# In a split-precision encoder block, operand groups are loaded behind the next weight pieces, and the work after each item gets a deadline

## The chip, the cores and the metric

The kernel runs on one core of one Trainium2 chip. The metric is device time in microseconds (us). The engines are named as in the profile: PE does matrix products (PEld is its weight load), DVE and ACT work on tiles, POOL and SP here issue transfers; L235 is line 235 of the kernel. "SPq", "POOLq" and "ACTq" stand for a transfer being issued by that engine's sequencer.

## The reference

One block of a streaming encoder over 512 tokens with 2048 channels, all in float32. An input projection feeds two mixers (a gated linear recurrence, mLSTM, and a short gated convolution), whose results go through two branch products, are merged by gates, and go through an output product; then a gated MLP of width 5504, with a short convolution between its products:

```python
hn = rmsnorm(h, norm_mix_g)
proj = hn @ w_in + b_in                                  # 2048 -> 11272
y_m = gate(mlstm(q, k, v, i, f)) @ w_branch_m            # 1024 -> 2048
y_c = (cb * causal_dwconv(cc * ch, conv_w)) @ w_branch_c # 1024 -> 2048
h = h + (sigmoid(gm) * y_m + sigmoid(gc) * y_c) @ w_out  # 2048 -> 2048
u = causal_dwconv(rmsnorm(h, norm_ffn_g) @ w_up, ffn_conv_w, ffn_conv_b)  # 2048 -> 2 * 5504
h = h + (silu(gate) * val) @ w_down                      # 5504 -> 2048
return rmsnorm(h, norm_out_g)
```

## The kernel before

Every large product is done in blocks by a seven-product (Strassen) scheme, and each float32 operand is split in two parts that PE can multiply: a high part (`hi`, an ACT copy) and the remainder (`lo`, a DVE subtraction). One product is then three matmuls, high by high (L279), high by low (L280) and low by high (L281), each 128x128 by 128x256.

The program is a list of **steps**. A step uses one **weight piece** (1 MB of combined weights in a slot of the ring `raw`): two halves, seven products each, 42 matmuls. An **item** is a run of steps (`q` = 0 to `nq` - 1) whose results collect in one set of PSUM banks; two items are interleaved at the start and at the end of each phase. The phases follow the reference: the input projection, `w_bc`, `w_bm`, `w_out`, `w_up`, `w_down` in three chunks of the inner width, and a short rest. I count pieces from 0 in a phase: `w_down.0` is the first of `w_down`. The phases meet at about 905 (into `w_bc`), 1060 (into `w_out`), 1245 (into `w_up`), 2140 (into `w_down`, first chunk), 2330 and 2455 us (second and third chunk).

**A weight piece** needs: two 128 KB loads on SP (L250, L251), two 128 KB loads on POOL that are added onto the first two once these have landed (L253), a 512 KB load on SP (L260); two sums on DVE (L216, L221); two high parts on ACT (L231); two low parts on DVE (L235), the second of which is the last use of the slot. In the last piece of some items ("eight") only the 512 KB load is there, the high parts are L184 and L185, the low parts L189 and L190.

**An operand group** (`cell_task`, `direct_cell`) is the activation side of a phase: two 256 KB loads of intermediate results from DRAM (L326), sums on DVE (L342 to L352; in `direct_cell` with L386 and L387 ahead), the high part on ACT (L356) and the low part on DVE (L359), which frees the slot. There are eight buffers (`ACTS`) for the finished groups, so the groups of a new phase are made while PE works at the seam of two phases, one every step or two.

Weight pieces and operand groups share the six slots of `raw` (`RAW`). `order` is the list of all of them in load order. SP works through it in that order: the n-th load is issued when the (n - 6)-th in the list has been used up. The list is made of `tasks[k]`, one list per step; an operand group whose work is to be done around step `k` is put ahead of weight piece `k`.

When an item ends, ACT copies the shared bank out (`evac_first`, L303) and DVE adds the other banks into a tile `z` (L309 to L312, `evac_ops`). Then come its **posts** (normalise, convolve, gate, store), put into the queue `posts` and worked off a few at a time when a running `credit` of DVE time allows. `flush` runs what is left of an older item's posts in one go when a later item ends, ahead of its L303: they read the tile `z` that L303 writes next. In the `up` phase the posts are L686 and L838 to L853 and the store into `a_d` (L148, issued by ACT); in the `down` phase L864 on ACT and an adding store into `h_d` (L155, issued by POOL).

Of the kernel before, what the change touches and what calls it, by code (L numbers as in the profile page):

```python
# [44 lines left out]
def kpair(c):  # L45

    q, r = divmod(c, 2)
    return 4 * q + r, 4 * q + 2 + r
# [12 lines left out]
class Task:  # L61


    def __init__(self, load, sums, hi, lo, ready=None):
        self.load, self.sums, self.hi, self.lo, self.ready = load, sums, hi, lo, ready
        self.wh = self.wl = None
        self.raw, self.cost, self.plain, self.after_end, self.pre = None, (0.8, 2.05), False, None, None


@with_exitstack  # L70
def tile_block(ctx: ExitStack, tc: tile.TileContext, xT, w1, w_v0, w_v1, w_v2, w_bm, w_bc, w_out, w_up, w_down,
# [13 lines left out]
    def nm(s):  # L85
        uid[0] += 1
        return f"{s}_{uid[0]}"
# [227 lines left out]
    def cell_task(xs, c, d, scale=None, key=None, eight=False):  # L315

        k1, k2 = kpair(c) if isinstance(c, int) else c
        t = Task(None, None, None, None)

        def new_raw():  # L320
            t.raw = wp.tile([P, NW], F32, tag="raw", name=nm("xraw"), bufs=RAW)

        def load():
            new_raw()
            for dst, k in zip(t.two(), (k1, k2)):
                SP.dma_start(dst, d[k])  # L326

        def two_k():
            return (t.raw[:, :T], t.raw[:, T:2 * T]) if eight else (t.raw[:, 5 * SW:], t.raw[:, :2 * SW])

        def scaled():
            for ap, k in zip(two_k(), (k1, k2)):
                A.activation(ap, ap, AF.Copy, scale=scale(k))

        def diff():
            x = slots(t.raw)
            V.tensor_sub(x[:, 4:6], x[:, 0:4:2], x[:, 1:4:2])

        def t3():
            x = slots(t.raw)  # L340

            V.tensor_sub(x[:, 2:4], x[:, 1:6:4], two(x[:, 6]))  # L342

        def e():

            x = slots(t.raw)
            V.scalar_tensor_tensor(x[:, 4], x[:, 3], -1.0, x[:, 1], op0=ALU.mult, op1=ALU.subtract)

        def t4():

            x = slots(t.raw)
            V.scalar_tensor_tensor(x[:, 6], x[:, 4], -1.0, x[:, 0], op0=ALU.mult, op1=ALU.subtract)  # L352

        def hi():
            t.act = actp.tile([P, 2 * NW], F32R, tag="act", name=nm("act"))
            A.activation(t.act[:, :m], t.raw[:, :m], AF.Copy)  # L356

        def lo():
            V.tensor_sub(t.act[:, NW:NW + m], t.raw[:, :m], f(t.act[:, :m]))  # L359
            t.raw = None  # L360
            xs[t.cell] = t.act
            t.act = None

        t.load, t.sums, t.hi, t.lo, t.new_raw = load, [diff] if eight else [t3, e, t4], hi, lo, new_raw
        t.two, m = two_k, 6 * SW if eight else NW
        t.pre = scaled if scale else None
        t.cost = (0.65, 1.7) if eight else (1.35, 1.95)
        t.ready = (lambda: all(k in stored for k in key)) if key else None
        return t

    def direct_cell(xs, c, it, d=None, scale=None, key=None, eight=False):

        t = cell_task(xs, c, d, None, key, eight)
        cell_t3, cell_load = t.sums[0], t.load
        k1, k2 = kpair(c)

        def load():
            if d is not None:
                cell_load()
            else:  # L380
                t.new_raw()

        def t3():
            assert it.done
            a, b = t.two()
            V.tensor_add(a, a, it.z[:, :T])  # L386
            V.scalar_tensor_tensor(b, it.z[:, T:], -1.0, b, op0=ALU.mult, op1=ALU.subtract)  # L387
            it.z_read = True
            cell_t3()

        def scaled():
            assert it.done
            for ap, z, k in zip(t.two(), (it.z[:, :T], it.z[:, T:]), (k1, k2)):
                A.activation(ap, z, AF.Copy, scale=scale(k))
            it.z_read = True

        it.z_read = False
        t.load = load
        if d is not None:
            t.sums = [t3] + t.sums[1:]  # L400
        else:
            t.pre = scaled
        t.cost = (t.cost[0] + (1.35 if d is not None else 0), t.cost[1])
        t.after_end = it
        return t
# [464 lines left out]
    steps, items_all, all_cells = [], [], []  # L870
# [190 lines left out]
    t = last_act()  # L1061
    t.cell, t.first, t.last, t.after, t.spread, t.xs = "x", e_last, e_last + 15, 0, e_last - 4, plain
    all_cells.append(t)
    n_main = len(steps)
    steps.extend((l, 0) for l in lasts)


    tasks = [[] for _ in range(len(steps) + 1)]
    wt = [weight_task(it, q) if isinstance(it, Item) else last_weight(it.n) for it, q in steps]
    k, cells_at = 0, {}  # L1070
    for n, t in enumerate(all_cells):
        if n < 8:
            k = t.cell
        else:
            k = max(k, all_cells[n - 8].last + 3, t.after, t.spread)
            if tasks[k]:
                k += 1
            t.k = k
            cells_at.setdefault(k, []).append(t)
            assert k <= t.first, (n, k, t.first)  # L1080
        tasks[k].append(t)
    for s, t in enumerate(wt):
        tasks[s].append(t)
    order = [t for ts in tasks for t in ts]
    place = {id(t): i for i, t in enumerate(order)}
    at = [place[id(t)] for t in wt] + [len(order) - 1] * 8
    n_load, n_lo, held = [0], [0], [0]

    def load_next():
        i = n_load[0]  # L1090
        if i == len(order) or i - n_lo[0] + held[0] == RAW or (order[i].ready and not order[i].ready()):
            return False
        order[i].load()
        n_load[0] += 1
        return True

    def loads():
        while load_next():
            pass
# [5 lines left out]
    def lo_ops(t):  # L1105

        def done():
            n_lo[0] += 1

        if isinstance(t.wh, list):  # L1110
            return [lambda: t.lo(0), lambda: (t.lo(1), done())]
        return [lambda: (t.lo(), done())]
# [123 lines left out]
    for i in range(at[START]):  # L1236
# [4 lines left out]
        while todo_mm:  # L1241
            s, r = todo_mm[0]
            it, q = steps[s]
# [41 lines left out]
    credit = 0.0  # L1285
    urgent = {it.num for it in items_all if it.urgent}


    finals, lq, lsum = deque(), [], []

    for s in range(START, len(steps)):
        it, q = steps[s]
# [89 lines left out]
        if s >= START + hold:  # L1382
            credit = min(credit, 2.5)
            rush = not main or any(x[0] in urgent for x in posts)
            for x in list(posts)[:2]:
                cost, fn = x[1][0]
                if not rush and cost and credit <= cost / 2:
                    break
                x[1].popleft()
                credit -= cost  # L1390
                fn()
                if not x[1]:
                    posts.remove(x)
        for t in cells_at.get(s + 3, []):
            if t.pre and t.raw is not None and (not t.after_end or t.after_end.done):
                t.pre()
                t.pre = None
# [10 lines left out]
        if not main and it.n > 11 and finals:  # L1408
            for _ in range(2):
                if finals:  # L1410
                    last_scale(0, finals.popleft(), row0)
        loads()
    for l in lq:
        last_post(l)
    for l in lsum + lq:
# [68 lines left out]
```

## Time and profile before

| | |
|---|---|
| time, median of 3 runs (lowest to highest) | 2645.81 us (2645.74 to 2651.76) |
| the profiled execution: its own time, its span | 2654.39 us, 2652.7 us |
| mean granted PE clock (1.00 is 2.4 GHz) | 0.99 |
| PE busy, share of the span, matmuls | 2584.3 us, 97%, 21146 |
| DVE, ACT, POOL busy | 2112.7, 1291.1, 796.4 us (80%, 49%, 30%) |
| DMA, mean over the span | 223 GB/s |

A matmul's duration in the trace is longer than its distance to the next one (they are pipelined): in undisturbed stretches one starts every 0.12 us. A stretch with n matmuls therefore has n x 0.12 us of work, and the rest of the stretch is lost, by waits or by a lower clock. Times in the views are counted from the start of the span.

### The profile page before, as it was taken

To read this page: it belongs to the slowest core of one execution; us is meant where nothing else is said; L and a number is where in the kernel's file an instruction comes from. 1 tells how busy PE (TensorE), PEld (TensorE's weight loads), DVE (VectorE), ACT (ScalarE), POOL (GpSimd) and SP (SyncE) were. 2 spreads that over 40 slices of the span, in tenths; PEclk is the share of its full clock that TensorE was granted. 3 is DMA by queue.
4 is the path that set the end of the run, shared out by engine and by line. 5 is a ranking of instruction groups with operands and counts; after the bars stand their busy time and mean duration, and the time that the engine had idled before them with its cause. 6 is when DMAs were issued, how large, how long until landed. Compare 5 with 4: busy or idle time off the path is not lost.

```text
span 2652.7 us, 55503 instructions
## 1 busy us (share of the span) xinstructions
PE 2584.3 (97%) x21146; PEld 2564.9 (97%) x21146; DVE 2112.7 (80%) x3308; ACT 1291.1 (49%) x1748; POOL 796.4 (30%) x922
## 2 busy tenths in 40 slices
PE   8999999999999999899999999999999989999998
PEld 8999999999999999899899999999999989999997
DVE  8577778886777888877989888888888887676756
ACT  6444554546556543345555445444444544444433
POOL 2443333333333111221333333333333223232320
PEclk8999999999999999999999999999999999999999
DMA  7798989998898797887998889989888888898976
GB/s 216 181 228 229 240 223 253 221 252 225 231 248 219 227 298 208 218 244 209 236 224 227 221 221 227 225 219 225 222 222 220 209 219 210 200 239 195 233 173 203
DMA packets 462557, 592.55 MB, mean 223 GB/s; under 512 B 42784, under 2 KB 296736, under 8 KB 462288
## 3 DMA queue, kind: packets, MB, share of 16 engines
q1 hardware_dynamic: 301968, 419.79, 50.4%
q0 software_dynamic: 133088, 124.04, 31.4%
q10 hardware_dynamic: 27232, 45.17, 4.7%
q8 instruction: 165, 2.70, 0.4%
q14 instruction: 104, 0.85, 0.1%
HBM read 531.17 MB, written 57.67 MB: 222 GB/s over the span
## 4 chain that ended last, share of the span: by engine, by line
PE 54%; DVE 6%; DMA 3%; issue 2%; ACT 0%; POOL 0%; DVEq 0%; SPq 0%; POOLq 0%; ACTq 0%
PE bank L281 18%; PE bank L279 18%; PE bank L280 17%; DMA raw<-in_w_down_dram 2%; DVE wl L235 1%; DVE act L359 1%; DMA raw<-in_w_out_dram 1%; DVE z L310 0%; PE bank L440 0%; PE bank L1164 0%; PE bank L1165 0%; PE bank L1166 0%; DMA raw<-in_w_up_dram 0%; DVE z L309 0%; DMA h_d<-z 0%
## 5 line engine op out<-in xcount | busy, mean ns | idle before, releaser
L281 PE MATMUL bank<-act,wl 128*128 128x256 f32 x6760 | 1922.7, 284 | 33.5 <-DVE wl L235 28.5
L279 PE MATMUL bank<-act,wh 128*128 128x256 f32 x6760 | 1931.1, 286 | 14.3 <-ACT z L303 5.8
L280 PE MATMUL bank<-act,wh 128*128 128x256 f32 x6760 | 1919.3, 284 | 0.0
L281 PEld LDWEIGHTS bank<-act,wl 128*128 128x128 f32 x6760 | 1303.9, 193 | 39.4 <-DVE wl L235 33.4
L279 PEld LDWEIGHTS bank<-act,wh 128*128 128x128 f32 x6760 | 1304.2, 193 | 18.8 <-ACT z L303 6.5
L231 ACT ACTIVATE wh<-raw 128x896 fp32r<-128x896 f32 x856 | 812.1, 952 | 1036.9 <-PE bank L280 679.5
L280 PEld LDWEIGHTS bank<-act,wh 128*128 128x128 f32 x6760 | 1304.3, 193 | 2.8 <-issue 1.7
L235 DVE TENSOR_TENSOR wl<-raw,wh 128x896 fp32r<-128x896 f32 x856 | 929.1, 1087 | 343.1 <-PE bank L281 231.7
L253 POOL DMA_DIRECT2D raw<-in_w_up_dram x344 | 298.5, 941 | 603.4 <-DMA raw<-in_w_up_dram 371.9
L253 POOL DMA_DIRECT2D raw<-in_w_dram x280 | 244.1, 961 | 527.1 <-DMA raw<-in_w_dram 344.9
L216 DVE TENSOR_TENSOR raw<-raw 128x256 f32<-128x256 f32 x428 | 179.6, 420 | 37.3 <-DMA raw<-in_w_down_dram 23.1
L253 POOL DMA_DIRECT2D raw<-in_w_down_dram x112 | 100.9, 1032 | 282.2 <-DMA raw<-in_w_down_dram 107.4
L221 DVE TENSOR_TENSOR raw<-raw 128x256 f32<-128x256 f32 x428 | 179.0, 418 | 0.3
L309 DVE TENSOR_TENSOR z<-bank,z 128x512 f32<-128x512 f32 x131 | 89.8, 686 | 38.4 <-ACT z L303 28.3
L356 ACT ACTIVATE act<-xraw 128x1792 fp32r<-128x1792 f32 (+1 forms) x52 | 85.6, 1646 | 60.2 <-DVE xraw L352 49.5
L184 ACT ACTIVATE wh<-raw 128x256 fp32r<-128x256 f32 x96 | 40.0, 416 | 131.0 <-PE bank L280 118.6
L359 DVE TENSOR_TENSOR act<-xraw,act 128x1792 fp32r<-128x1792 f32 (+1 forms) x52 | 101.7, 1955 | 0.0
L686 DVE TENSOR_TENSOR z<-z,rstd 128x1024 f32<-128x1024 f32 x83 | 100.8, 1217 | 0.2 <-ACT rstd L457 0.2
L189 DVE TENSOR_TENSOR wl<-raw,wh 128x256 fp32r<-128x256 f32 x96 | 40.5, 421 | 64.3 <-PE bank L281 37.3
L310 DVE TENSOR_TENSOR z<-bank,z 128x512 f32<-128x512 f32 x131 | 89.6, 684 | 1.7
L312 DVE TENSOR_TENSOR z<-bank,z 128x512 f32<-128x512 f32 x131 | 89.5, 683 | 0.0
L253 POOL DMA_DIRECT2D raw<-in_w_out_dram x48 | 41.8, 983 | 131.5 <-DMA raw<-in_w_out_dram 91.0
(214 smaller groups left out, 1380.3 us busy)
## 6 DMA issues: line engine op xcount, KB each, us to landing
raw<-in_w_up_dram SPq DMA_DIRECT2D x172, 512.0 KB, 5.7
raw<-in_w_dram SPq DMA_DIRECT2D x144, 512.0 KB, 5.9
raw<-in_w_up_dram SPq DMA_DIRECT2D x344, 128.0 KB, 3.9
raw<-in_w_up_dram POOLq DMA_DIRECT2D x344, 128.0 KB, 5.4
raw<-in_w_down_dram SPq DMA_DIRECT2D x80, 512.0 KB, 5.1
raw<-in_w_dram SPq DMA_DIRECT2D x280, 128.0 KB, 4.3
raw<-in_w_dram POOLq DMA_DIRECT2D x280, 128.0 KB, 5.4
raw<-in_w_out_dram SPq DMA_DIRECT2D x32, 512.0 KB, 5.2
```

The lines of the kernel that those rows point to most:

```text
L216: V.tensor_add(x[:, 6], x[:, 5], x[:, 0])
L221: V.tensor_add(x[:, 2], x[:, 6], x[:, 1])
L231: A.activation(seven(t.wh[r]), half(r), AF.Copy)
L235: V.tensor_sub(seven(t.wl[r]), half(r), seven(f(t.wh[r])))
L253: G.dma_start(at(i), a21, accum_op=ALU.add)
L279: PE.matmul(ps, h, xh, start=start, stop=False, skip_group_check=True)
L280: PE.matmul(ps, h, xl, start=False, stop=False, skip_group_check=True)
L281: PE.matmul(ps, l, xh, start=False, stop=stop, skip_group_check=True)
L309: return [lambda: V.tensor_add(z[:, 0:4:3], b0, two(z[:, 1])), lambda: V.tensor_add(z[:, 1:3], b1, two(z[:, 3])), lambda: V.tensor_add(z[: ...
L310: lambda: V.tensor_add(z[:, 1:3], b1, two(z[:, 3])),
L359: V.tensor_sub(t.act[:, NW:NW + m], t.raw[:, :m], f(t.act[:, :m]))
L686: V.tensor_mul(sb_pair(it.z), sb_pair(it.z), two(rstd))
```

## The change

Three edits. (1) In `order`, an operand group no longer stands ahead of the weight piece of its step `k` but `behind` steps later: 2 in general, 1 for groups from a load that are scaled first, 3 for groups that are made from `z` without a load. The step at which its work on DVE and ACT is done stays. Which loads may be issued is now counted along the list with a flag `done`, since groups and pieces may be used up out of the list's order. (2) A post is also run when its item's remaining posts are as many as the steps left until `due`, the end of the item whose evacuation needs the tile. (3) `loads()` stands ahead of two later parts of the loop's body. (`for t in cells_at.get(s + 3, [])` scales groups early on ACT.)

```diff
 class Task:
+        self.done, self.behind = False, 2
 def cell_task(...):
-        t.pre = scaled if scale else None
+        if scale:
+            t.pre, t.behind = scaled, 1
 def direct_cell(...):
         else:
-            t.pre = scaled
+            t.pre, t.behind = scaled, 3
...
-    k, cells_at = 0, {}
+    low, cells_at = 0, {}
     for n, t in enumerate(all_cells):
         if n < 8:
             k = t.cell
         else:
-            k = max(k, all_cells[n - 8].last + 3, t.after, t.spread)
-            if tasks[k]:
+            k = max(low, all_cells[n - 8].last + 3, t.after, t.spread)
+            if k in cells_at:
                 k += 1
-            t.k = k
+            t.k = low = k
             cells_at.setdefault(k, []).append(t)
             assert k <= t.first, (n, k, t.first)
+            k = min(k + t.behind, len(steps))
         tasks[k].append(t)
...
     def load_next():
         i = n_load[0]
+        while n_lo[0] < i and order[n_lo[0]].done:
+            n_lo[0] += 1
...
         def done():
-            n_lo[0] += 1
+            t.done = True
...
+    ends = {it.num: s for s, (it, q) in enumerate(steps[:n_main]) if q == it.nq - 1}
+
+    def due(num):
+
+        n = num + 2
+        return ends.get(n if n < len(items_all) and (n < 42 or items_all[n].pre) else n + 1, len(steps))
...
-                if not rush and cost and credit <= cost / 2:
+                if not rush and cost and credit <= cost / 2 and len(x[1]) < due(x[0]) - s:
                     break
...
+        loads()
         for t in cells_at.get(s + 3, []):
...
-        loads()
```

PE's rows stand in the same order before and after. Three places where others move are shown; lines of the kernel after are one or two higher.

**SP at the seam into `w_down`**, before: an operand group (from `a_d`), the last piece of `w_up`, a group, `w_down.0`, and the first two rows of `w_down.1`.

```order
L326 DMA xraw_25251<-a_d 128x512 x2
L250 DMA raw_25309<-in_w_up_dram 128x256
L251 DMA raw_25309<-in_w_up_dram 128x256
L260 DMA raw_25309<-in_w_up_dram 128x2x512
L326 DMA xraw_25315<-a_d 128x512 x2
L250 DMA raw_25375<-in_w_down_dram 128x256
L251 DMA raw_25375<-in_w_down_dram 128x256
L260 DMA raw_25375<-in_w_down_dram 128x2x512
L250 DMA raw_25439<-in_w_down_dram 128x256
L251 DMA raw_25439<-in_w_down_dram 128x256
L260 DMA raw_25439<-in_w_down_dram 128x2x512
```

The same place after:

```order
L251 DMA raw_25188<-in_w_up_dram 128x256
L252 DMA raw_25188<-in_w_up_dram 128x256
L261 DMA raw_25188<-in_w_up_dram 128x2x512
L327 DMA xraw_25254<-a_d 128x512 x2
L251 DMA raw_25312<-in_w_down_dram 128x256
L252 DMA raw_25312<-in_w_down_dram 128x256
L261 DMA raw_25312<-in_w_down_dram 128x2x512
L327 DMA xraw_25375<-a_d 128x512 x2
L251 DMA raw_25378<-in_w_down_dram 128x256
L252 DMA raw_25378<-in_w_down_dram 128x256
L261 DMA raw_25378<-in_w_down_dram 128x2x512
```

The groups shown before are the third and the fourth of this phase, and after the second and the third: the last piece of `w_up` and `w_down.0` each have two groups fewer ahead of them, and so come two places earlier in the ring. The same happens at the other seams; 74 rows of SP's list differ in all.

**DVE near 2195 us**, at the end of an item of `w_down`, before: low parts of a weight piece, then six posts of one item of `up` (L686 to L853 on `z_92`), and the evacuation of the next item, which writes `z_92` (L309).

```order
L235 TENSOR_TENSOR wl_26045<-raw_25829,wh_25971 128x896
L312 TENSOR_TENSOR z_93<-bank_86,z_93 128x512
L235 TENSOR_TENSOR wl_26048<-raw_25829,wh_26030 128x896
L686 TENSOR_TENSOR z_92<-z_92,rstd 128x1024
L842 SCALAR_TENSOR_TENSOR mB<-z_92,pcol,mB 128x511
L843 SCALAR_TENSOR_TENSOR mB<-z_92,pcol,mB 128x510
L846 SCALAR_TENSOR_TENSOR mB<-z_92,pneg,mB 128x511
L847 SCALAR_TENSOR_TENSOR mB<-z_92,pneg,mB 128x510
L853 TENSOR_TENSOR mB<-mB 128x512
L216 TENSOR_TENSOR raw_25897<-raw_25897 128x256
L309 TENSOR_TENSOR z_92<-bank_80,z_92 128x2x256
```

After, from the fourth row of the evacuation before it on:

```order
L236 TENSOR_TENSOR wl_26051<-raw_25829,wh_25972 128x896
L313 TENSOR_TENSOR z_93<-bank_86,z_93 128x512
L236 TENSOR_TENSOR wl_26054<-raw_25829,wh_26027 128x896
L848 SCALAR_TENSOR_TENSOR mB<-z_92,pneg,mB 128x511
L849 SCALAR_TENSOR_TENSOR mB<-z_92,pneg,mB 128x510
L855 TENSOR_TENSOR mB<-mB 128x512
L217 TENSOR_TENSOR raw_25959<-raw_25959 128x256
L310 TENSOR_TENSOR z_92<-bank_80,z_92 128x2x256
```

Between the last low part and the evacuation three posts are left; the other three (L686, L842 and L843 of before) stand earlier, ahead of the evacuation of `z_93`.

**ACT near 2212 to 2235 us**, in the same chunk, before: L864 (the `down` post) of `z_93`, then high parts, and L864 of `z_92`.

```order
L864 ACTIVATE z_93<-z_93 128x512
L231 ACTIVATE wh_26240<-raw_25960 128x896
L231 ACTIVATE wh_26288<-raw_25960 128x896
L838 ACTIVATE mA<-z_91,pcol 128x512
L839 ACTIVATE mA<-z_91,pcol,pneg 128x512
L864 ACTIVATE z_92<-z_92 128x512
```

After:

```order
L185 ACTIVATE wh_26428<-raw_26178 128x256
L186 ACTIVATE wh_26428<-raw_26178 128x256
L185 ACTIVATE wh_26475<-raw_26178 128x256
L186 ACTIVATE wh_26475<-raw_26178 128x256
L866 ACTIVATE z_93<-z_93 128x512
L866 ACTIVATE z_92<-z_92 128x512
L232 ACTIVATE wh_26491<-raw_26235 128x896
L232 ACTIVATE wh_26540<-raw_26235 128x896
L866 ACTIVATE z_91<-z_91 128x512
L232 ACTIVATE wh_26553<-raw_26296 128x896
L304 ACTIVATE z_93<-bank_83 128x256
```

L866 (L864 of before) of `z_93` and `z_92` now stand together, behind the high parts of an "eight" piece and 15 and 11 rows later in the list; five rows behind the second, L304 (L303 of before) writes `z_93` anew.

## Rows read from the trace of the kernel before

**Rows 1.** The page's line on each engine: busy us, share of the span, instructions.

```profile
PE 2584.3 (97%) x21146; PEld 2564.9 (97%) x21146; DVE 2112.7 (80%) x3308; ACT 1291.1 (49%) x1748; POOL 796.4 (30%) x922
```

**Rows 2.** Windows at seams of phases and at the end of items: length, then busy time and instructions of each engine, the granted PE clock, the DMA engines' busy share, GB/s.

```profile
880.00:920.00 40.00, 37.49 (x311) 37.09 (x310) 34.69 (x48) 19.07 (x25) 7.00 (x8) 1.00 0.75 217
1020.00:1060.00 40.00, 36.63 (x301) 36.02 (x301) 39.51 (x62) 17.86 (x26) 5.22 (x6) 1.00 0.70 201
1060.00:1120.00 60.00, 53.19 (x418) 52.09 (x417) 52.33 (x75) 23.64 (x32) 12.18 (x14) 0.94 0.78 211
1240.00:1310.00 70.00, 62.98 (x489) 61.73 (x488) 63.04 (x100) 42.34 (x53) 18.99 (x22) 0.95 0.83 221
2120.00:2180.00 60.00, 52.36 (x414) 51.14 (x413) 52.44 (x70) 30.19 (x34) 14.02 (x16) 0.97 0.79 207
2180.00:2210.00 30.00, 25.33 (x200) 25.13 (x199) 23.71 (x38) 11.91 (x19) 8.71 (x10) 0.94 0.88 235
2435.00:2475.00 40.00, 37.03 (x291) 36.39 (x290) 31.26 (x48) 18.96 (x24) 7.04 (x8) 0.96 0.78 203
```

**Rows 3.** What PE waited for, over the whole span: engine and line that waited, what ended the wait, us in total, times, the longest.

```profile
PE bank L281 <- DVE wl L235: 28.5, 21, 2.5
PE bank L279 <- ACT z L303: 5.8, 3, 4.7
PE bank L279 <- DVE z L309: 2.9, 1, 2.9
```

**Rows 4.** The chain of work that ended last, at the seam into `w_down`: start, length, what.

```profile
2128.43 3.83 DMA raw<-in_w_down_dram
2132.61 0.46 POOL raw L253
2133.15 5.99 DMA raw<-in_w_down_dram
2140.64 0.58 PE bank L281
```

**Rows 5.** Timeline of SP at the same seam: start, length of the issue, what is loaded. In order: the last piece of `w_up`, the fourth group of this phase, `w_down.0`, `w_down.1`.

```profile
2121.53 0.33 SPq L250 DMA_DIRECT2D raw<-in_w_up_dram  x1
...
2123.46 0.80 SPq L326 DMA_DIRECT2D xraw<-a_d  x2
2127.58 0.33 SPq L250 DMA_DIRECT2D raw<-in_w_down_dram  x1
...
2133.09 0.33 SPq L250 DMA_DIRECT2D raw<-in_w_down_dram  x1
```

**Rows 6.** Timeline of DVE: sums (L216) that waited for a late weight piece, at the seams into `w_bc` (`w_bc.1`), `w_out` (`w_out.5`), `w_up` (`w_up.0`), the first chunk of `w_down` (`w_down.0`) and the third (`w_down.56`), in brackets the idle time and what ended it; and last the first sum (L342) on the fourth group of [rows 5].

```profile
902.49 0.43 DVE L216 TENSOR_TENSOR raw<-raw 128x256 f32<-128x256 f32 x1 [3.60 <-DMA raw<-in_w_bc_dram]
...
1113.43 0.42 DVE L216 TENSOR_TENSOR raw<-raw 128x256 f32<-128x256 f32 x1 [2.27 <-DMA raw<-in_w_out_dram]
...
1256.92 0.42 DVE L216 TENSOR_TENSOR raw<-raw 128x256 f32<-128x256 f32 x1 [3.84 <-DMA raw<-in_w_up_dram]
...
2139.16 0.42 DVE L216 TENSOR_TENSOR raw<-raw 128x256 f32<-128x256 f32 x1 [2.77 <-DMA raw<-in_w_down_dram]
...
2451.11 0.43 DVE L216 TENSOR_TENSOR raw<-raw 128x256 f32<-128x256 f32 x1 [4.51 <-DMA raw<-in_w_down_dram]
...
2141.84 0.68 DVE L342 TENSOR_TENSOR xraw<-xraw 128x512 f32<-128x512 f32 x1
```

**Rows 7.** Timeline of SP at the seams into `w_bc` (`w_bc.0` and `w_bc.1`), into `w_up` (a group from `h_d`, then `w_up.0`) and into the third chunk of `w_down` (the last piece of the second, an "eight" one, then `w_down.56`).

```profile
885.13 0.33 SPq L250 DMA_DIRECT2D raw<-in_w_bc_dram  x1
...
893.27 0.33 SPq L250 DMA_DIRECT2D raw<-in_w_bc_dram  x1
1242.25 0.80 SPq L326 DMA_DIRECT2D xraw<-h_d  x2
...
1244.87 0.33 SPq L250 DMA_DIRECT2D raw<-in_w_up_dram  x1
2433.55 0.38 SPq L260 DMA_DIRECT2D raw<-in_w_down_dram  x1
...
2438.59 0.33 SPq L250 DMA_DIRECT2D raw<-in_w_down_dram  x1
```

**Rows 8.** Timelines of DVE (the first, the fourth and the sixth of the six posts) and ACT (L303, which writes `z_92`) at the end of an item.

```profile
2195.39 1.22 DVE L686 TENSOR_TENSOR z<-z,rstd 128x1024 f32<-128x1024 f32 x1
...
2198.95 0.74 DVE L846 SCALAR_TENSOR_TENSOR mB<-z,pneg,mB 128x511 f32<-128x511 f32 x1
...
2200.58 0.69 DVE L853 TENSOR_TENSOR mB<-mB 128x512 f32<-128x512 f32 x1
...
2201.68 0.38 ACT L303 ACTIVATE z<-bank 128x256 f32<-128x256 f32 x1 [1.92 <-DVE raw L216]
```

**Rows 9.** Transfers issued from 2120 to 2175 us: tile, issuing engine, count, size of one, median us from issue to landing.

```profile
xraw<-a_d SPq DMA_DIRECT2D x10, 256.0 KB, 5.1
raw<-in_w_down_dram POOLq DMA_DIRECT2D x12, 128.0 KB, 5.9
```

**Rows 10.** Timeline of ACT after 2230 us: the last row of an "eight" piece, and the L303 that writes `z1` (`z_93` above).

```profile
2233.73 0.40 ACT L185 ACTIVATE wh<-raw 128x256 fp32r<-128x256 f32 x1
2242.23 0.37 ACT L303 ACTIVATE z<-bank 128x256 f32<-128x256 f32 x1
```

**Rows 11.** The adding stores from `z` to `h_d` between 2200 and 2260 us, four of them: from issue to landing.

```profile
DMA to landing us min/median/max: 6.4/8.1/9.8
```

## The prediction

> **What bounds the kernel now.** I read the page first. PE is busy for 97% of the span [rows 1], so only PE's waits and its clock can be won; DVE stands next at 80%, with the sums and low parts that each weight piece needs before PE may use it. The table of waits [rows 3] then says what PE waits for: 28.5 us in 21 waits for L235, the low part of a weight piece, 5.8 us in 3 for L303, ACT's copy that opens an evacuation.
>
> Where these waits stand is seen in windows [rows 2]. A stretch with n matmuls has n x 0.12 us of work, so its loss is its length less that: 40 - 311 x 0.12 = 2.7 us at the seam into `w_bc`, 3.9 into `w_bm` (1020 to 1060), 9.8 into `w_out`, 11.3 into `w_up`, 10.3 into `w_down`, 6.0 at the end of an item (2180 to 2210), 5.1 into the third chunk. That is 49 us, and it is the pool from which this change can draw, since its edits move rows only there. Part of each loss is the clock. A mean of 0.97 over 60 us means 2 x 0.03 x 60 = 3.6 us at 1.2 GHz instead of 2.4, half of which, 1.8 us, is lost. In these windows the clock is below 1.00 only where PE also waited long; the windows into `w_bc` and `w_bm`, where PE's waits were short, show 1.00 [rows 2].
>
> Why L235 is late is told by the chain [rows 4] and by the idle time of DVE [rows 6]. `w_down.0` is issued at 2127.58 [rows 5]. Its SP loads land 3.83 us after 2128.43, only then does POOL issue the added loads at 2132.61, and these take 5.99 us: DVE gets the piece at 2139.14, after 2.77 us of idling, and PE goes on at 2140.64. So a load takes 11.6 us in two legs, one behind the other, and DVE waits for it. The same wait costs DVE 3.60 us at `w_bc.1`, 2.27 at `w_out.5`, 3.84 at `w_up.0` and 4.51 at `w_down.56` [rows 6].
>
> **The change part by part.** *Order of loads.* No load is added or removed; the n-th load still waits for the end of the (n - 6)-th. A piece that has two groups fewer ahead gets the slot that was given out two places earlier. At `w_down.0` that is the one at which the last piece of `w_up` was issued, 2121.53 instead of 2127.58, so 6.1 us earlier; `w_bc.1` gets that of `w_bc.0`, 885.13 instead of 893.27, 8.1 earlier; `w_down.56` moves from 2438.59 to 2433.55, 5.0 earlier; `w_up.0` only one place, from 1244.87 to 1242.25, 2.6 earlier [rows 5, 7]. Both legs move with the issue, as POOL's order of pieces stays. Except at `w_up.0`, the lead is longer than DVE's wait [rows 6].
>
> What is won, seam by seam, bounded above by the loss [rows 2] and by DVE's idle time in the window, as DVE's own work doesn't shrink:
>
> - into `w_bc`: the wait of 3.60 us is covered by the lead of 8.1, so nearly the whole loss: 2.5 (0 to 2.7).
> - into `w_bm`: DVE is busy 39.5 of 40 us [rows 2]; no wait to take away: 0.
> - into `w_out`: only `w_out.5` waits long for its load; 2.27 plus a little for a smaller one, 2.5. The longest stall there, 2.9 us, is for L309 of an evacuation [rows 3] and stays. Bounds 0 and 6.
> - into `w_up`: of 3.84 us at most 2.6 can go; I take 2.0 for PE, and half of the clock's loss (0.05 x 70 = 3.5) on top, 1.7: 3.7 (0.5 to 5.5).
> - into `w_down`: DVE works 52.4 of 60 us while PE's work is 49.7. The stretch can't get shorter than DVE's work unless that starts before 2120, so 60 - 52.4 = 7.6, not the 10.3 lost. The lead of 6 us at `w_down.0`, and the like at the four pieces after it, is enough for that: 7.6 (4 to 10.3).
> - into the third chunk: 5.0 us of lead against 4.51 of waiting, DVE idle 8.7 in all: 4.7 of the 5.1 (2 to 5.1).
>
> Together 21.0 us.
>
> *Posts by a deadline.* At the end of the item at 2202 us six posts stand on DVE in one burst from 2195.39 to 2201.2, and L303 can't write `z_92` before the last of them has read it and its store is issued: it starts at 2201.68 [rows 8], and PE waits 4.7 us [rows 3]. After, the first three of the six stand ahead of the evacuation before. The fourth started at 2198.95 [rows 8], so what is left starts 3.56 us earlier. I take 3.3 of the 4.7 for PE, and with a stall of only some 1.4 us left the clock's loss of 0.06 x 30 = 1.8 goes too (1.7): 5.0 (0 to 6.0). The other two waits for L303, 5.8 - 4.7 = 1.1 us, are of this kind and should go: 1.1. The moved posts cost DVE nothing new: between 2180 and 2210 it idles 6.3 us [rows 2]. If that cover were gone they would delay a low part by up to their 3.56 us.
>
> *What is late next.* Groups now come later. The fourth group of `w_down` was issued at 2123.46; after, `w_down.0`, another group and `w_down.1` go first and it gets the slot of 2133.09, 9.6 us later [rows 5]. A group's load takes 5.1 us [rows 9], so it lands at 2138.2; DVE took it up at 2141.84 [rows 6], and will want it at 2139.1 when the wait of 2.77 is gone. That leaves 0.9 us. I charge 1 us in all for groups that come a little late (0 to 6). Second, L864 of `z1` and `z0` now comes behind the "eight" piece that ended at 2234.1 [rows 10]. Its adding store starts near 2235 and takes 6.4 to 9.8 us [rows 11], so it ends between 2241 and 2245, and L303, which overwrites `z1`, was at 2242.23 [rows 10]. ACT may wait 0 to 2.6 us there, with high parts of the next pieces behind it and DVE's low parts behind those: 1 us (0 to 2.6). *The moved `loads()`* issues loads ahead of ACT's early scaling; SP's own rows are all there is to move: 0.
>
> Sum: 21.0 + 5.0 + 1.1 - 1 - 1 = 25.1 us. The profiled execution of 2654.4 us would take 2629.3. It is 8.6 us above the median of the runs, and the terms are waits in us, so I take them off the median in full: 2645.8 - 25.1 = 2620.7, **2621 us**.
>
> **The rivals.** *Half at the seams.* Earlier loads overlap with others. POOL's leg took 5.9 us for 128 KB where SP's groups took 5.1 for 256 KB [rows 9], so it already suffers from company, and groups now follow right behind the pieces, into that leg. Against it: the DMA engines were busy for only 0.75 to 0.83 of the time at the seams [rows 2]. If half of the 21.0 goes, 10.5 more remain: 2631. The Trainium skill (DMA: Bandwidth & Descriptors, "Queues, rings and completion order") says that each DMA engine takes turns, packet by packet, between the queue rows that it has work for. By that rule SP's loads slow POOL's leg whatever their place in SP's order; the row of POOL's 5.9 us agrees with it, and no row before the change separates it from POOL's own work of issuing.
>
> *DVE is the bound.* In the window into `w_down` DVE's work already exceeds PE's, 52.4 against 49.7 us. If the waits that go at a seam come back as waits for L235 some steps later, only the posts' part stays, 6.1 less 1: 2641, within 0.3%. Against it: from 2180 to 2210 DVE idles 6.3 us, so it catches up.
>
> *Slower: groups too late.* Each of seven seams has some three groups that move by 7 us or more. DVE takes its work in order, so a group that hasn't landed stops the low parts of the pieces behind it, and PE soon after. The spare time is 0.9 us, as worked out above. If groups took 3 us longer than 5.1, 21 groups x 2.1 us = 44 us would be lost: 2665. It turns the sign when the mean wait is over 25.1 / 21 = 1.2 us, so with loads of 7.2 us. For it: stores of the same queues take up to 9.8 us [rows 11]. Against it: 5.1 is the median in a stretch that is already crowded.
>
> *All of it.* If DVE runs far enough ahead for the whole loss at the changed places to go (49 less the 3.9 into `w_bm`): 2600.
>
> **How the numbers follow.** Forecast (2611 to 2629) 0.55, half 0.20, DVE-bound 0.13, slower 0.05, nearly all 0.07. A difference under 0.3%, 7.9 us, can't be told from none here: below 2638 is faster, and that is 0.55 + 0.20 + 0.07 = 0.82; the same 0.13; slower 0.05. The range leaves out the DVE-bound and the slower case and the far end of the last: 2608 to 2638.
>
> **What would show it.** Right: in the windows of [rows 2], 414 matmuls in some 52 us into `w_down`; no wait of DVE for a raw piece at `w_bc.1`, `w_down.0` and `w_down.56`, and PE's waits for L235 down from 28.5 to about 12 us; the wait of 4.7 for L303 down to 1 or 1.5; clock 1.00 there. Wrong: PE's sum for L235 unchanged with DVE busy throughout (DVE-bound); DVE waiting for `xraw` from `a_d`, `h_d` or `mc_d` (late groups); L303 near 2242 waiting for the store into `h_d`; POOL's leg well above 5.9 us (half). What I can't see is how far the new order of groups shifts DVE's work against PE's, which is where an error of 10 us would sit.

## The result: 0.7% faster, some three quarters of what was forecast

Measured in the same runs, the kernel before takes 2648.27 us (median of 6) and the changed kernel 2630.38 us (median of 6, 2626.63 to 2635.24): a ratio of 0.9929, with a 95% interval from 0.9911 to 0.9947. By the ratio that is 18.8 us less (14 to 24), by the two medians 17.9. The forecast was 25.1 us less, 2621 us. The measured time lies inside the range of 2608 to 2638, but above the forecast's own 2611 to 2629 and at the 2631 of the rival "half at the seams"; the time alone can't tell these two apart, the seams below can. The profiled execution went from 2654.39 to 2635.24 us, 19.2 us less, and that is the pair of traces compared here.

The page's line on the engines, and the waits of PE that answer to [rows 3] (L236 is L235 of before, L310 is L309, L304 is L303):

```profile
PE 2579.5 (98%) x21146; PEld 2562.4 (97%) x21146; DVE 2112.6 (80%) x3308; ACT 1291.9 (49%) x1748; POOL 799.5 (30%) x922
```

```profile
PE bank L282 <- DVE wl L236: 16.7, 13, 2.7
PE bank L280 <- DVE z L310: 3.9, 2, 2.2
PE bank L280 <- ACT z L304: 1.0, 1, 1.0
```

The waits for the low parts fell from 28.5 us in 21 waits to 16.7 in 13, and the wait of 4.7 us for L303 to one of 1.0. Against this, PE now waits 3.9 us for L310, the opening addition of an evacuation, where it waited 2.9.

Since PE's rows stand in the same order in all these kernels, the time between the same two matmuls can be compared. Stretches between the seams that the change doesn't touch repeat to 0.01 us (the 6583 matmuls from 1320 to 2110 us take 789.96 us in each of the 14 traces), so small differences at the seams can be read. The start of the program does not repeat so: the matmuls up to 850 us took 849.4 us in the changed kernel's profile and 844.5 in a second one. The table is worked out from the starts of the matmuls, the first column by times of before; `order_only` and `deadline_only` are two experiments (below).

| us | before | changed | difference | forecast | `order_only` | `deadline_only` |
|---|---|---|---|---|---|---|
| into `w_bc`, 880 to 930 | 50.07 | 47.04 | -3.0 | -2.5 | 47.04 | 51.14 |
| into `w_bm`, 1012 to 1062 | 49.97 | 49.90 | -0.1 | 0 | 49.98 | 49.89 |
| into `w_out`, 1062 to 1150 | 88.05 | 85.18 | -2.9 | -2.5 | 85.18 | 87.33 |
| an item's end, 1150 to 1200 | 49.99 | 49.08 | -0.9 | - | 49.99 | 49.08 |
| into `w_up`, 1243 to 1320 | 77.09 | 80.04 | **+3.0** | **-3.7** | 79.38 | 76.17 |
| into `w_down`, 2110 to 2182 | 71.99 | 65.16 | -6.8 | -7.6 | 65.17 | 70.25 |
| an item's end, 2182 to 2215 | 33.07 | 28.04 | -5.0 | -5.0 | 32.97 | 28.60 |
| an item's end, 2215 to 2240 | 24.94 | 24.00 | -0.9 | -1.1 with the last row | 24.95 | 24.00 |
| into the second chunk, 2310 to 2345 | 35.03 | 34.19 | -0.8 | - | 33.91 | 35.96 |
| into the third chunk, 2430 to 2480 | 50.08 | 46.39 | -3.7 | -4.7 | 46.39 | 50.39 |
| an item's end, 2480 to 2505 | 24.97 | 24.24 | -0.7 | see above | 24.24 | 26.15 |

The differences add up to -22.0; +2.4 us more at the start and the end of the program (0.7 ahead of 850 us and 1.7 behind 2620), where the change moves no row, make the -19.6 by which the last matmul starts earlier.

Windows of before and of the changed kernel over the same matmuls (into `w_bc`, `w_up`, `w_down`, the item's end at 2202 us, the third chunk; columns as in [rows 2]), before:

```profile
880.00:930.07 50.07, 47.56 (x395) 47.16 (x393) 43.54 (x62) 25.94 (x35) 8.72 (x10) 1.00 0.80 237
1243.00:1320.10 77.10, 70.08 (x544) 68.35 (x543) 68.86 (x112) 45.74 (x58) 22.76 (x27) 0.96 0.88 231
2120.00:2182.04 62.04, 54.40 (x431) 53.18 (x430) 53.63 (x74) 31.72 (x36) 14.22 (x17) 0.97 0.80 209
2182.04:2215.11 33.07, 28.40 (x226) 28.20 (x224) 26.19 (x43) 12.58 (x20) 10.56 (x13) 0.95 0.82 220
2430.00:2480.08 50.08, 47.11 (x375) 46.47 (x374) 40.59 (x60) 26.22 (x36) 10.19 (x12) 0.97 0.75 194
```

and changed:

```profile
880.72:927.76 47.04, 47.04 (x395) 47.04 (x393) 44.49 (x64) 27.04 (x38) 8.50 (x10) 1.00 0.87 255
1236.84:1316.88 80.04, 71.57 (x544) 69.53 (x542) 70.18 (x114) 45.85 (x58) 24.38 (x28) 0.94 0.86 227
2116.80:2172.00 55.20, 52.25 (x432) 51.64 (x431) 54.24 (x72) 32.25 (x37) 13.14 (x15) 1.00 0.86 227
2172.00:2200.04 28.04, 27.00 (x226) 26.80 (x225) 27.24 (x48) 12.76 (x21) 7.94 (x10) 1.00 0.94 249
2413.14:2459.53 46.39, 45.02 (x376) 44.82 (x374) 40.59 (x60) 26.46 (x36) 10.99 (x13) 1.00 0.84 220
```

DVE's busy time is the third of the sums. Into `w_down` DVE's work was 53.6 of 62.0 us and is 54.2 of 55.2: the stretch is now nearly as long as DVE's work. At 2172 it is 27.2 of 28.0. The clock is 1.00 at all places where the waits are gone, and 0.94 into `w_up`.

Why `w_up` is different is seen in the chain of work there:

```profile
1243.42 3.85 DMA raw<-in_w_up_dram
1247.83 0.52 POOL raw L254
1248.37 9.25 DMA raw<-in_w_up_dram
1257.98 0.68 DVE z L310
```

`w_up.0` is in time now. But the next piece, `w_up.1`, comes late in its place: issued at 1243.42, its POOL leg takes 9.25 us, DVE waits 4.25 us for it, and L310 stands behind that sum in DVE's order. SP's timeline shows what is issued around it (the pieces `w_up.1` and `w_up.2`, the residual of an item of `w_out`, 512 KB, and a group from `h_d`):

```profile
1243.42 0.33 SPq L251 DMA_DIRECT2D raw<-in_w_up_dram  x1
...
1246.19 0.33 SPq L251 DMA_DIRECT2D raw<-in_w_up_dram  x1
...
1247.52 0.47 SPq L757 DMA_DIRECT2D mA<-in_xT_dram  x1
1248.95 1.43 SPq L327 DMA_DIRECT2D xraw<-h_d  x2
```

The end of the item that was at 2202 us, on DVE: last low part, the three posts that are left, then the evacuation, one after the other without the six-post burst of [rows 8].

```profile
2184.26 1.08 DVE L236 TENSOR_TENSOR wl<-raw,wh 128x896 fp32r<-128x896 f32 x1
2185.26 0.75 DVE L848 SCALAR_TENSOR_TENSOR mB<-z,pneg,mB 128x511 f32<-128x511 f32 x1
2186.04 0.75 DVE L849 SCALAR_TENSOR_TENSOR mB<-z,pneg,mB 128x510 f32<-128x510 f32 x1
2186.90 0.69 DVE L855 TENSOR_TENSOR mB<-mB 128x512 f32<-128x512 f32 x1
2187.51 0.42 DVE L217 TENSOR_TENSOR raw<-raw 128x256 f32<-128x256 f32 x1
2188.41 0.69 DVE L310 TENSOR_TENSOR z<-bank,z 128x512 f32<-128x512 f32 x1 [0.49 <-ACT z L304]
```

### The profile page after: what moved, and what is told of

Its sections match the earlier page's. It is cut to its first block, busy times and chain, and to the rows that moved or that the text cites. A ratio compares the mean times of both kernels' runs of the same rounds, so it can differ in the third digit from the quotient of the medians.

```text
span 2633.5 us, 55501 instructions
## 1 busy us (share of the span) xinstructions
PE 2579.5 (98%) x21146; PEld 2562.4 (97%) x21146; DVE 2112.6 (80%) x3308; ACT 1291.9 (49%) x1748; POOL 799.5 (30%) x922
## 4 chain that ended last, share of the span: by engine, by line
PE 70%; DVE 4%; issue 1%; DMA 1%; ACT 0%; SPq 0%; DVEq 0%; POOL 0%; ACTq 0%; POOLq 0%
PE bank L282 22%; PE bank L280 22%; PE bank L281 22%; DVE wl L236 1%; DVE act L360 1%; DMA raw<-in_w_up_dram 1%; PE bank L1170 0%; PE bank L442 0%; PE bank L1171 0%; PE bank L1172 0%; PE bank L639 0%; DVE z L311 0%; DVE raw L217 0%; DVE z L310 0%; DVE xraw L343 0%
## 5 line engine op out<-in xcount | busy, mean ns | idle before, releaser
L282 PE MATMUL bank<-act,wl 128*128 128x256 f32 x6760 | 1920.5, 284 | 20.1 <-DVE wl L236 16.7
L236 DVE TENSOR_TENSOR wl<-raw,wh 128x896 fp32r<-128x896 f32 x856 | 930.3, 1088 | 343.8 <-PE bank L282 232.9
L310 DVE TENSOR_TENSOR z<-bank,z 128x512 f32<-128x512 f32 x131 | 89.9, 687 | 34.7 <-ACT z L304 23.1
```

The source lines that it names most:

```text
L236: V.tensor_sub(seven(t.wl[r]), half(r), seven(f(t.wh[r])))
L282: PE.matmul(ps, l, xh, start=False, stop=stop, skip_group_check=True)
L310: return [lambda: V.tensor_add(z[:, 0:4:3], b0, two(z[:, 1])), lambda: V.tensor_add(z[:, 1:3], b1, two(z[:, 3])), lambda: V.tensor_add(z[: ...
```

## The experiments

**The parts.** The first kernel keeps the order and leaves out the deadline, the second the other way round.

```diff
 # order_only
-                if not rush and cost and credit <= cost / 2 and len(x[1]) < due(x[0]) - s:
+                if not rush and cost and credit <= cost / 2:
 # deadline_only
-            k = min(k + t.behind, len(steps))
```

> The new load order with the done flags and the moved loads, posts as before. If the two parts add, it keeps the seams: -3.0 us into w_bc, -2.9 into w_out, +2.9 into w_up, -6.8 into w_down, -3.7 into the third chunk (each the shift of the same matmul against before, as measured in the whole change), and gives nothing at the ends of items at 2202, 2225 and 2496 us. About 12 us faster than before (2636). If the posts are what spoils the seam into w_up, that seam gains 2 to 4 us here instead of losing 2.9, and the time is near 2630.

> Posts by a deadline, groups ahead of the weight piece as before. If the parts add: -5 us at the end of the item at 2202 us, -0.9 at 2225, -0.7 at 2496, -0.9 between 1150 and 1200, nothing at the seams; 7 us faster than before (2641). If the posts are what spoils the seam into w_up, that seam gets some 3 us longer here too.

`order_only` took 2634.64 us (ratio 0.9945, 0.9924 to 0.9966), `deadline_only` 2643.61 (0.9979, 0.9968 to 0.9990); 2636 and 2641 were expected. The product of the ratios is 0.9924, the whole change 0.9929: the parts add within these intervals. The table above says where each acts: the seams into `w_bc`, `w_out`, `w_down` and the third chunk belong to the order, the item's ends at 2202 and 2225 us to the deadline, to 0.1 us or 0.6. Two places were put down wrongly in the expectation: the end at 2496 us follows the order of loads (24.24 with it, 26.15 with the deadline alone), and the seam into `w_up` is spoilt by the order, not by the posts: 79.4 with the order alone, 76.2 with the deadline alone. With the deadline alone nothing was expected at the seams, but six of them moved by 0.3 to 1.7 us, both ways.

**The late piece at the seam into `w_up`.** Two explanations were at hand: `w_up.1` got no lead, or its POOL leg is slow for what is transferred beside it. `scaled_behind_2` gives it a lead, which also parts its POOL leg from the loads of `w_up.2`; `no_residual_load` takes the residual out of the company (and the additions that need it); `residual_a_step_later` moves the residual and leaves nothing out.

```diff
 # scaled_behind_2, and once more as scaled_2_again
-            t.pre, t.behind = scaled, 1
+            t.pre, t.behind = scaled, 2
 # no_residual_load (and in out_post: if p < 6: residual(it))
-                it.pre(it)
+                if it in out_items[6:]:
+                    it.buf = (mA, mB)[it.num % 2]
+                else:
+                    it.pre(it)
 # residual_a_step_later
-                it.pre(it)
+                if it in out_items[6:]:
+                    late.append(lambda it=it: it.pre(it))
+                else:
+                    it.pre(it)
```

> The changed kernel, but the groups loaded from h_d stand two steps behind instead of one, so that w_up.1 gets its slot one place earlier (4.7 us, from 1243.4 to 1238.7). If the wait at the seam into w_up only moved from w_up.0 to w_up.1 for want of lead, DVE's wait of 4.25 us for w_up.1 goes and PE's waits of 2.17 and 1.89 us there with it: 3 to 6 us less than the changed kernel at this seam. If the added loads of POOL are slow there because of what is transferred beside them, the wait stays at 2 us or more, on whichever piece.

> The changed kernel without the two residual loads (512 KB each, from the input) of the last two items of w_out, which SP issues at 1247.5 and 1254.8 us, between pieces of w_up; the additions of these residuals are left out too (four DVE rows). If POOL's added load for w_up.1 (9.25 us from issue to landing in the changed kernel, 6.5 before) is slow because of company, it falls to 6 to 7 us and DVE's wait of 4.25 us falls to 1 to 2. If it is slow for another reason, both stay as they are.

> The changed kernel with the two residual loads of the last two items of w_out issued one step later, nothing left out. If company is what slows POOL's added load for w_up.1, the first residual load no longer runs beside it: 6 to 7.5 us instead of 9.25, DVE's wait for it 1 to 2 us instead of 4.25, the seam into w_up 2 to 4 us shorter. If the effect of leaving these loads out came from the additions left out, the seam stays.

The company slows the leg. The transfers that POOL issued for `w_up.1` (tile, engine, count, size, median us to landing), in the changed kernel:

```profile
raw<-in_w_up_dram POOLq DMA_DIRECT2D x2, 128.0 KB, 8.8
```

and with the residual a step later:

```profile
raw<-in_w_up_dram POOLq DMA_DIRECT2D x2, 128.0 KB, 6.0
```

Without the residual loads it is 6.5, in the changed kernel's second profile 7.7. DVE's wait for the piece falls with it, from 4.25 us (2.75 in the second profile) to 0.9.

The residual is only half of the company. Before the change it was there too: it was issued at 1253.20 us, and POOL's leg for `w_up.1`, 6.8 us long, at 1253.70. What is new is `w_up.2`, whose loads now start 1.6 us ahead of that leg; before they came 5.4 us behind it. The 14 traces agree on this. The slower of POOL's two transfers takes 8.5 to 9.3 us in the six in which both the residual and `w_up.2` are issued beside the leg, 6.2 to 7.4 in the five with the residual and a later `w_up.2`, 7.3 and 7.4 in the two with `w_up.2` alone, and 5.0 in the one with neither (`all_behind_3`). So beside the other, either of them costs POOL's 128 KB some 1 to 2 us. For the residual `residual_a_step_later` shows it; for `w_up.2` it is read from kernels that differ in more than that.

The Trainium skill (DMA: Bandwidth & Descriptors, "Queues, rings and completion order") has each DMA engine take turns between the queue rows that it has work for. The traces agree in that loads issued by SP slow the leg issued by POOL; the turns themselves are not seen in them.

But with the residual later the seam got no shorter, 80.90 us against 80.04. DVE's waits there:

```profile
DVE z L792 <- DMA mB<-in_xT_dram: 2.9, 1, 2.9
DVE raw L217 <- DMA raw<-in_w_up_dram: 0.9, 1, 0.9
```

The 2.9 us for the residual, which is now late itself, took the place of the wait for the weight piece. The expectation of 2 to 4 us less failed. Without the residual loads the seam took 75.42 us, but there four additions of 0.69 us are left out too, so this run doesn't say how much is due to the loads.

`scaled_behind_2` took 2626.46 us (0.9912, 0.9895 to 0.9930). DVE waits for no weight piece at this seam any more, and it takes 76.97 us: 3 less than changed, as expected, but no less than before (77.09), although before DVE waited 5.0 us for pieces there (3.84 and a smaller one). So something else bounds it.

**What bounds the seam into `w_up`.** The third of the groups' sums is left out, in the changed kernel and in `scaled_behind_2`; the latter and the changed kernel were timed again side by side.

```diff
 # fewer_sums_up; fewer_sums_up_scaled_2 has behind = 2 as above too
+    def cut(t):
+        t.sums = t.sums[:2]
+        return t
-          HH, [direct_cell(HH, c, out_items[c], None, g_ffn) if c > 4 else
-               cell_task(HH, c, h_d, g_ffn, [("h", c)]) for c in range(8)], (-4, -2, -1, 0, 2, 3, 4, 5))
+          HH, [cut(direct_cell(HH, c, out_items[c], None, g_ffn) if c > 4 else
+                   cell_task(HH, c, h_d, g_ffn, [("h", c)])) for c in range(8)], (-4, -2, -1, 0, 2, 3, 4, 5))
```

> The same kernel as scaled_behind_2, timed beside the changed kernel on one chip. If the 3.1 us that its profile showed at the seam into w_up (76.97 against 80.04 us for the same matmuls) are its own, it is 2 to 5 us faster than the changed kernel. If they are the scatter of that seam from run to run (the same program took 80.0 and 78.2 us there in two profiles), the two medians are within 1.5 us.

> The changed kernel once more, for the comparison with scaled_2_again: 0.990 to 0.994 of before. Its seam into w_up again takes 78 to 80 us, with POOL's added load for w_up.1 at 8.9 us or more.

> The changed kernel without the third sum (L353, 0.42 us) of the eight groups of w_up, 3.4 us of DVE work in all, of which six groups are made inside the seam. If the late w_up.1 bounds this seam, its length stays at 78 to 80 us. If DVE's own work bounds it, it falls by 2 to 4 us, to 75 to 77.

> The same left out of scaled_behind_2, where DVE no longer waits for any weight piece at the seam into w_up. DVE's work bounds what is left there (65.3 us of DVE work in 72, PE's work 60.2): the seam falls from 77.0 by 2 to 4 us, more if the clock is restored with it. If PE waits there for something that is no work of DVE (the sum that goes through PE and the groups' scaling on ACT), it falls by less than 1 us.

Windows over the same matmuls, first `deadline_only`, then `scaled_2_again`, `fewer_sums_up` and `fewer_sums_up_scaled_2`:

```profile
1239.06:1315.23 76.17, 69.93 (x543) 68.29 (x542) 70.26 (x114) 45.79 (x58) 24.40 (x28) 0.96 0.88 237
```

```profile
1231.84:1308.82 76.98, 68.92 (x543) 66.89 (x542) 70.09 (x114) 46.07 (x58) 24.33 (x28) 0.98 0.89 236
```

```profile
1232.85:1309.99 77.14, 69.74 (x543) 67.79 (x542) 67.15 (x106) 45.97 (x58) 24.37 (x28) 0.96 0.88 234
```

```profile
1235.61:1309.83 74.22, 69.84 (x544) 68.27 (x543) 67.08 (x106) 46.18 (x58) 24.36 (x28) 0.95 0.91 245
```

PE's work is 541 x 0.12 = 64.9 us in each, DVE's 67 to 70. The length is DVE's work plus DVE's idle time, and one can add it up ("scaling" is DVE's wait for ACT to scale a group, L396 and L334):

| us | length | DVE's work | DVE idle | of that for a weight piece | for scaling |
|---|---|---|---|---|---|
| before | 77.1 | 68.9 | 8.2 | 5.0 | 0 |
| changed | 80.0 | 70.2 | 9.9 | 4.3 | 2.3 |
| changed, second profile | 78.5 | 70.2 | 8.3 | 2.8 | 2.3 |
| `deadline_only` | 76.2 | 70.3 | 5.9 | 2.6 | 0 |
| `all_behind_1` (below) | 77.4 | 69.7 | 7.7 | 3.5 | 1.0 |
| `scaled_2_again` | 77.0 | 70.1 | 6.9 | 0 | 3.6 |
| `fewer_sums_up` | 77.1 | 67.2 | 10.0 | 4.1 | 2.0 |
| `fewer_sums_up_scaled_2` | 74.2 | 67.1 | 7.1 | 0 | 3.3 |

3 us less of DVE's work makes the seam 2.8 us shorter in `scaled_behind_2`, as that theory said. In the changed kernel, where a piece is late, it is 2.9 us shorter against the profile with nearly the same wait for the piece (4.3 and 4.1 us) and 1.4 against the second. The expectation gave this as a choice, the late piece or DVE's work; the two add up in DVE's order, so both count. These are single profiles of a seam that scatters by 1.5 us from profile to profile.

And an idle time that is taken away can come back under another name: `scaled_2_again` has none for pieces, but 3.6 us for scaling, and the changed kernel 2.3, of which before shows none in this stretch. DVE's waits for scaling in the changed kernel:

```profile
DVE xraw L343 <- ACT xraw L396: 1.3, 1, 1.3
DVE xraw L343 <- ACT xraw L334: 1.0, 1, 1.0
```

and in `scaled_2_again`:

```profile
DVE xraw L343 <- ACT xraw L396: 2.6, 2, 1.3
DVE xraw L343 <- ACT xraw L334: 1.0, 1, 1.0
```

They come from the order: `deadline_only`, in which no group is moved, has none, and with one step for every group the one for L396 (groups made from `z`) is gone.

The two medians side by side are 2627.0 us for `scaled_2_again` (0.9915, 0.9902 to 0.9929) and 2630.11 for `changed_again` (0.9925, 0.9911 to 0.9938). `scaled_behind_2` is the best of the versions that leave nothing out: 3 us in the medians, with overlapping intervals, so not shown by the times alone; the seam itself took 77.0 us in both of its profiles against 80.0 and 78.5. The leg of 8.9 us or more that was expected in `changed_again` was 8.7 at its slower transfer.

**How far behind.** One number for every group, 1 or 3, in place of 2, 1 and 3.

```diff
-        self.done, self.behind = False, 2
+        self.done, self.behind = False, 1        # all_behind_3: 3
-        if scale:
-            t.pre, t.behind = scaled, 1
+        if scale:
+            t.pre = scaled
-            t.pre, t.behind = scaled, 3
+            t.pre = scaled
```

> The changed kernel with every group one step behind, none two or three. Half the lead: if the gain at a seam follows the lead until DVE's wait is covered, the seams into w_bc and w_down keep most of it (DVE's waits of 3.6 and 2.8 us against leads of some 3 to 5), into the third chunk about half is lost (4.5 us of waiting against some 3). 2 to 5 us slower than the changed kernel, all of it at those seams. If the lead beyond one place is worth nothing, the seams are those of the changed kernel within 0.5 us.

> The changed kernel with every group three steps behind. The rival of late groups says: each group comes 3 to 5 us later than in the changed kernel, where the spare time was about 1 us, so DVE waits 2 to 4 us for some three groups at each of seven seams, 20 us or more slower than the changed kernel, and DVE's waits for xraw stand in the table of waits. If groups have more spare time than that, the time stays within 3 us; the seam into w_up then gains as with two steps, some 3 us.

With 1, the time, measured once, is 2631.43 us, 1 more than the changed kernel's median where 2 to 5 were expected. The seam into the third chunk takes 48.30 us (46.39 changed, 50.08 before), because the first piece is late again, by 2.7 us instead of 4.5 before and 0 after:

```profile
2433.60 0.42 DVE L217 TENSOR_TENSOR raw<-raw 128x256 f32<-128x256 f32 x1 [2.68 <-DMA raw<-in_w_down_dram]
```

Into `w_down` it is 1.4 us longer than changed and into the second chunk 1.2, into `w_bc` the same: there half the lead is enough. The seam into `w_up` is shorter than changed, 77.4 us, which was not expected. With 3 the time, measured once, is 2647.92 us, some 17 more than the changed kernel's median (20 or more were expected) and nearly that of before (2650.84 beside it). This is one step further for the groups from `a_d`, two for those from `h_d`. DVE's waits over the whole span (engine, line, what ended the wait, us, times, longest):

```profile
DVE xraw L343 <- DMA xraw<-a_d: 11.5, 8, 2.2
DVE xraw L343 <- ACT xraw L334: 8.0, 3, 5.1
DVE xraw L338 <- DMA xraw<-a_d: 2.8, 1, 2.8
```

Here are the late groups of the rival: 14.3 us of waiting for groups from `a_d`, and 8.0 for ACT's scaling (L334) of groups from `h_d`, 5.1 at once. ACT in turn waits for their loads, from 1225 to 1260 us:

```profile
ACT xraw L334 <- DMA xraw<-h_d: 5.7, 2, 3.1
```

The seam into `w_up` takes 85.3 us, into `w_down` 69.9 and the end of the item behind it 32.5. Had the groups had more spare time, 3 us were expected to be gained into `w_up`; it lost 5.

**DVE as the bound into `w_down`.**

```diff
+            if c == 0:
+                cells[-1].sums = cells[-1].sums[:2]
```

> The changed kernel, from which the third sum (L353, 0.42 us on DVE) of the six seven-product groups of the first chunk of w_down is left out, 2.5 us of DVE work in all. If DVE's own work is what bounds that seam now (52.3 us of DVE work in the 53 us that 413 matmuls take there, PE's work 49.6), the two waits of PE for L236 of 1.26 and 1.57 us shrink by nearly 2.5 us together and the seam with them. If late loads still bound it, nothing moves.

```profile
2108.51:2162.59 54.08, 52.00 (x432) 51.59 (x430) 52.20 (x67) 32.24 (x37) 13.65 (x16) 1.00 0.86 232
```

The stretch fell from 55.2 to 54.1 us, DVE's work from 54.2 to 52.2 (five of the six sums lie in it). About half of the work left out came back as time: DVE is the first bound there, and another stands close behind it. Which one was not tried. PE's two waits fell from 2.8 us to 2.1 together, where nearly 2.5 less was expected.

## Why the prediction was nearly right, and where it was wrong

- *Moved loads.* Right at the seams into `w_bc` (3.0 for 2.5), `w_out` (2.9 for 2.5), `w_down` (6.8 for 7.6) and not into `w_bm` (0.1 for 0). Taking DVE's idle time, not PE's loss, as the cap into `w_down` held: 0.96 us of DVE's idle time is left in 55.2. `order_only` shows these gains without the deadline.
- *Third chunk*, 3.7 for 4.7: DVE's wait for the piece went, and one of 0.8 us for a late group came. That is the charge of 1 us for late groups.
- *Posts by a deadline*, 5.0 for 5.0 at 2202 us, and `deadline_only` shows it alone. The 1.1 for the two other waits was 1.7 (0.94 + 0.73), but at one of the two, at 2496 us, by the order of loads. That wait was not of this kind: before, L303 there waited for an adding store, not for posts:

```profile
2495.64 0.38 ACT L303 ACTIVATE z<-bank 128x256 f32<-128x256 f32 x1 [4.16 <-DMA h_d<-z]
```

- *Not in the sum*: 0.9 us at 1160 and 0.8 into the second chunk, which the prediction doesn't mention.
- *The adding store* was late as worked out: ACT waits 2.5 us for it (0 to 2.6 was said). PE lost nothing, so the charge of 1 us was too high:

```profile
2228.86 0.39 ACT L304 ACTIVATE z<-bank 128x256 f32<-128x256 f32 x1 [2.54 <-DMA h_d<-z]
```

- **The step that failed** is the term *into `w_up`*: "of 3.84 us at most 2.6 can go; I take 2.0 for PE, and half of the clock's loss". It measured +3.0 and, in a second profile, +1.4, against -3.7. Three things take the place of the gain. The lead of a piece was weighed alone: `w_up.1` gets no lead, and `w_up.2`, moved up beside it, made its POOL leg 8.8 us in place of 6.8, so the wait went from one piece to the next (5.0 us of waiting before, 4.3 and 2.8 after). That is the mechanism of the rival "half at the seams", at one seam and with the whole gain instead of half. The groups that now come later made DVE wait 2.3 us for their scaling, for which the sum has only the 1 us charged for all late groups. And DVE's work in this stretch is 1.3 us more (two more rows). Work and waits of DVE add up to the length here, so with all piece waits gone and the other two there, the seam is as long as before. The cap that held into `w_down` would not have shown it: in the window of [rows 2] DVE idles 7.0 us, more than the 3.7.
- *Luck in the sum.* The table's -22.0 is 3.1 us short of 25.1, though the term into `w_up` alone is 6.7 short. The rest came out 3.6 us better than said: 1.7 from places that were not mentioned, and 2 from the charges, which are in the measured terms already where they came at all.
- *The slower rival* didn't come at the chosen distances, where DVE waits 1.0 us for groups from `a_d` in two waits; one step further it does, and takes nearly the whole gain. The spare time of 0.9 us was right for the fourth group of `w_down`: its load lands 0.86 us ahead of its first sum in the changed kernel. But that is a tight one: of the 20 groups of `w_down`, 5 have about 1.5 us or less and the others 3 to 12, so loads 3 us longer would have delayed a quarter of these groups, not all. Its "stores of the same queues" are issued by POOL, the groups' loads by SP.

## What to carry over

In a shared ring with in-order slots, loading the later-needed operand behind the next weights is worth DVE's wait at that place, and one place too far loses it again: read the spare time of the moved load first. Cap each stretch by the idle time of the engine that feeds the bound one, but don't take the cap for the gain: a wait that goes can come back as the wait for what was moved behind. Ask of a transfer that is moved up not only when it lands but which one it then runs beside. When the bound engine's order doesn't change, compare the time between the same two of its instructions; that reads tenths of a microsecond where medians scatter by several.

## What was not expected of the hardware

- A 128 KB adding load issued by POOL landed after 3.2 to 9.3 us in one stretch of 25 us of the changed kernel (1239 to 1264 us, eight loads). This scatter is larger than the lead of 2.6 us that was given to `w_up.0`; for `w_up.1`, what was issued beside it goes with 5.0 to 9.3 us over the 14 traces.
- The same program differs at a crowded seam from run to run: 80.0 and 78.5 us for the same 541 matmuls, with waits for `w_up.1` of 4.3 and 2.8 us. The seam into `w_down`, where DVE waits for no load, took 65.16 and 65.17 us in the same two profiles.
